# A fused two-layer decoder trunk: most columns of the first feed-forward matrix by rows, transposed by a transfer instead of by TensorE

## The chip, the cores and the metric

The kernel runs on one core of one Trainium2 chip. The metric is device time in microseconds (us) for one execution of the whole program, weights read from HBM. TensorE is called PE in the profile, VectorE DVE, ScalarE ACT, GpSimd POOL and SyncE SP. L223 is line 223 of the kernel before; a name ending in q (ACTq) is an engine's instruction queue issuing a transfer.

## The reference

256 tokens of width 1024 go through two layers. Each layer is a feed-forward half-step, a mixer (spatial gating and differential attention) and a second feed-forward half-step, with a layer norm after each:

```python
def _swiglu(x, w1, w3, w2):
    return (jax.nn.silu(x @ w1) * (x @ w3)) @ w2
...
for l in range(DEPTH):                                   # DEPTH = 2
    h = _swiglu(x, ffn_w1[l, 0], ffn_w3[l, 0], ffn_w2[l, 0])
    x = _layernorm(ALPHA * x + 0.5 * h, ln_g[l, 0], ln_b[l, 0])
    h = _mixer(x, l, w_in[l], ...)
    x = _layernorm(ALPHA * x + h, ln_g[l, 1], ln_b[l, 1])
    h = _swiglu(x, ffn_w1[l, 1], ffn_w3[l, 1], ffn_w2[l, 1])
    x = _layernorm(ALPHA * x + 0.5 * h, ln_g[l, 2], ln_b[l, 2])
```

The inner width of the feed-forward networks (FFNs) is 2816, 22 tiles of 128 columns. There are four FFNs in all. Only their first product, `silu(x @ w1) * (x @ w3)`, and what depends on its layout is touched here.

## The kernel before

Every fp32 product is made of three products of reduced parts: an operand is split into a high part (`ACT` copies it into a rounded type, L169 for weights and L176 for activations) and a low part (`DVE` subtracts, L171 and L177), and PE computes hi x hi, hi x lo and lo x hi into one PSUM bank. Weights come from HBM in 1 MB tiles `raw` (4 slots, transfers issued by SP) and are split in pieces of 128x1024 into `hi` and `lo` slots (8 of each), so that PE has up to eight pieces waiting for it. PSUM has four main banks (`bank`) and four side banks (`side_bank`, `sbank` in the profile), each set taken in turn.

A first product is computed in one of two ways.

- By columns (`gemm_a2`, L223 and L230): the weight tile is the stationary operand, the moving one is `x_cat`, all 256 tokens with high and low parts side by side, 512 wide; then the low weights against the high half, 256 wide. The result stands with the inner columns on partitions, which is what the product with `w2` needs. For each of the four banks of a pair of column tiles ACT copies the second half of the bank out (`r`, L231), and DVE adds the first half to it (L233); then follow silu (L599), the product (L603 or L607) and the split.
- By rows (`gemm_first` or `gemm_b2`, with `rows_b` and `three`, L211): 128 tokens of x are stationary, 512 columns of weights move, three products each. One block of four column tiles is 96 such matmuls. The result stands with tokens on partitions and has to be transposed: `front` computes silu and product for one half `t` of the tokens, and `turned` transposes it on PE, four matmuls against the identity (L585), into a side bank, from which it is split.

Before the change, column tiles 0 to 3 come by rows and tiles 4 to 21 by columns, in nine pairs.

The product with `w2` follows (the w2 stage). Four of the pairs of tiles, `SQ` = (4,5), (6,7), (8,9), (10,11), go through a Strassen-like scheme: `mixed` makes sums of the activations, `stream_s` sums of the weights (`shi`, `slo`; L293, L295, L306 to L309), and seven products `S[1]` to `S[7]` are accumulated, three matmuls each, S[3], S[7] and S[4] in side banks and the others in main banks. The rest, `PQ`, is multiplied plainly and accumulated into the same banks and one more side bank. After the first pair's seven products a plain pair follows, and so on.

Order: PE's instructions are issued as the program writes them. On ACT, DVE, POOL and SP a scheduler sorts the work by due times that it derives from PE's program (`step`, `beat` advance that clock; `beside(g, n)` puts a generator's work n units later in it), and the result is a fixed order: an engine that waits for one instruction does not run the next one. Transfers that an engine issues stand in the same order.

Of the kernel before, what the change touches and what calls it, by code (L numbers as in the profile page):

```python
# [12 lines left out]
F32R = mybir.dt.float32r  # L13
BF16 = mybir.dt.bfloat16
I32 = mybir.dt.int32
AF = mybir.ActivationFunctionType
ALU = mybir.AluOpType
AX = mybir.AxisListType

P = 128  # L20
D = 1024
T = 256
# [31 lines left out]
def trunk(ctx, tc, x, xT, w13a, w13b, w2s, w2p, wb, wqk, wa, wbr, wo, gateb, sgug, sgub, sguwT, sgubias, lam, diffg,  # L54
# [81 lines left out]
    def beside(task, delay):  # L136
        tasks.append([clock[0] + delay, task])
# [72 lines left out]
        for n, (w, xx) in enumerate([(w_hi, xh), (w_lo, xh), (w_hi, xl)]):  # L210
            PE.matmul(ps, xx, w, start=start and n == 0, stop=stop and n == 2)  # L211

    def gemm_a2(srcs, xc, zs, rs=lambda: s512("r"), scale=1.0):

        b, got = [], []
        for src in srcs:
            got += stream(src)
            for hi, _ in got[-2:]:  # L220
                b.append(bank())
                for k in range(KT):
                    PE.matmul(b[-1], hi[:, k * P : (k + 1) * P], xc(k), start=k == 0, stop=False)  # L223
                beat(0.65)
        for n, (_, lo) in enumerate(got):
            s = slice(n % 2 * T, (n % 2 + 1) * T)
            if n % 2 == 0:
                r, z = rs(), zs(n // 2)
            for k in range(KT):
                PE.matmul(b[n][:, :T], lo[:, k * P : (k + 1) * P], xc(k)[:, :T], start=False, stop=k == KT - 1)  # L230
            emptied[0] = A.activation(r[:, s], b[n][:, T:], AF.Copy, scale=scale).ins  # L231
# [85 lines left out]
    def gemm_b2(srcs, xh, xl, done, norm=None):  # L317
# [233 lines left out]
    def ffn(l, f, i, norm, last=False):  # L551
        xh, xl = parts(both)
        h_hi, h_lo = ({q: act.tile([P, 512], F32R, tag="slot", name=name(n)) for q in PQ} for n in ("hhi", "hlo"))
        f_hi, f_lo = ([d[k, k + 1] for k in range(0, FB, 2)] for d in (h_hi, h_lo))
# [21 lines left out]
        def front(t, ps):  # L576
            s = t512("silu")
            A.activation(s, ps[0], AF.Silu)
            V.tensor_tensor(out=s, in0=s, in1=ps[1], op=ALU.mult)
            beside(turned(t, s), 2)  # L580

        def turned(t, s):
            b = side_bank()
            for k in range(FB):
                PE.transpose(b[:, k * P : (k + 1) * P], s[:, k * P : (k + 1) * P], ident)  # L585
            b4 = b.rearrange("p (k t) -> p k t", k=4)
            for j in range(2):
                hi, lo = (v.rearrange("p (k t) -> p k t", k=2)[:, :, t * P : (t + 1) * P] for v in (f_hi[j], f_lo[j]))
                split(hi, lo, b4[:, 2 * j : 2 * j + 2])
            yield 0  # L590

        if norm is None:
            gemm_first([w13b[l, f, 0], w13b[l, f, 1]], front)
        else:
            gemm_b2([w13b[l, f, 0], w13b[l, f, 1]], xh, xl, front, norm=norm)
        for j in range(FB, FT, 2):
            for m, z in gemm_a2([w13a[l, f, j - FB + m] for m in range(2)], both, lambda m: t512("silu")):
                s = z[:, :T]
                silu[0] = A.activation(s, s, AF.Silu).ins  # L599
                if (j, j + 1) in SQ:  # L600
                    if m == 0:
                        qa = s512("qa")
                    V.tensor_tensor(out=qa[:, m * T : (m + 1) * T], in0=s, in1=z[:, T:], op=ALU.mult)  # L603
                    if m:
                        mixed((j, j + 1), qa)
                else:
                    V.tensor_tensor(out=s, in0=s, in1=z[:, T:], op=ALU.mult)  # L607
                    split(hh(j + m), hl(j + m), s)
                if norm is None and j + m == FB:
                    beside(setup(s[:, :1]), 0)  # L610
        ln = Norm(l, i, 2.0 * ALPHA, 4.0 * EPS, s[:, :1], last)
# [46 lines left out]
    def mixer(l, i, norm):  # L658
# [34 lines left out]
        def attend(hp, qT, kT):  # L693
# [7 lines left out]
            def exps(t):  # L701
# [7 lines left out]
                pp = []  # L709
                for m in range(2):  # L710
                    o = m * 4 + t * 2
                    p = s512("pp", 4)[:, : 2 * nk]
# [118 lines left out]
        def spatial(gp, uu):  # L831
            b = side_bank()
            for j in range(2):
                g = gp * 2 + j
                s = slice((g % 4) * P, (g % 4 + 1) * P)
                for t in range(NT):
                    PE.matmul(b[:, j * T + t * P : j * T + (t + 1) * P], vg[t][:, g // 4, s], wsT[g // 4][:, s],  # L837
                               start=True, stop=True)
            s1 = s512("sgu", 4)
# [51 lines left out]
def _layout(i):  # L891
# [30 lines left out]
    nb = FB * P  # L922
    w1, w3 = f["ffn_w1"], f["ffn_w3"]
    o["w13a"] = c(np.stack([cols(w1[..., nb:]), cols(w3[..., nb:])], axis=4)).reshape(L, 2, FT - FB, P, CH)
    o["w13b"] = c(np.concatenate([halves(w1[..., :nb]), halves(w3[..., :nb])], axis=2))
    w2 = f["ffn_w2"].reshape(L, 2, FT, P, 2, 512)

    def blocks(at):
# [45 lines left out]
```

## Time and profile before

| | |
|---|---|
| time, median of three runs | 1230.99 us (1230.78 to 1231.02) |
| the profiled execution's own time | 1231.23 us |
| its span in the profile | 1229.5 us |
| PE busy | 1223.3 us, 99%, 6589 matmuls |
| DVE busy | 980.3 us, 80% |
| ACT busy | 781.1 us, 64% |
| POOL busy | 87.0 us, 7% |
| moved by transfers | 241.87 MB, mean 197 GB/s |
| granted PE clock | full in all 40 slices |

The profile is one execution. Busy times are shares of the span; the chain of waits names the work that ended last at each moment; a windows view cuts the span into stretches. In the FFNs' rows a pair of column tiles appears as 32 matmuls of L223 and 32 of L230, a block by rows as 96 of L211.

### The profile page before, as it was taken

Reading aid. Unit: us, or ns where it says so; the run is one execution under the profiler, and the core shown is the slowest. Engines: PE = TensorE matmul, PEld = TensorE weight load, DVE = VectorE, ACT = ScalarE, POOL = GpSimd, SP = SyncE. Lnnn points to the kernel's source line nnn. Section 1 sums busy time; section 2 is a strip of 40 time slices with the busy share of each in tenths; the row PEclk is TensorE's granted clock in tenths of the full one; section 3 lists DMA queues with packets and bytes.
Section 4 is the critical chain, followed back from the end, with each engine's and each line's share of the span. In section 5 each row is a group of like instructions: output and inputs, shape, how many; then the busy total and the mean of one; then the engine's idle time right before and its main releaser. Section 6 shows DMA issues by size and latency. Waiting matters only on the chain.

```text
span 1229.5 us, 17890 instructions
## 1 busy us (share of the span) xinstructions
PE 1223.3 (99%) x6589; PEld 1050.6 (85%) x6589; DVE 980.3 (80%) x1692; ACT 781.1 (64%) x1424; POOL 87.0 (7%) x184
## 2 busy tenths in 40 slices
PE   9999999999999999999999999999999999999998
PEld 8888888888888888888888888888888888888886
DVE  6877998886587987779978779978866879787886
ACT  6775666679665666656566665566886555766651
POOL 0100000244100000000000000002430000000000
PEclk9999999999999999999999999999999999999999
DMA  9864665654754745546645546656556446455450
GB/s 344 291 205 138 231 217 194 224 167 166 251 178 154 231 159 207 191 138 241 247 178 196 180 142 247 246 188 206 168 174 229 168 171 240 171 206 178 160 211 34
DMA packets 40104, 241.87 MB, mean 197 GB/s; under 512 B 5281, under 2 KB 6353, under 8 KB 13393
## 3 DMA queue, kind: packets, MB, share of 16 engines
q1 hardware_dynamic: 36048, 227.82, 53.2%
q0 software_dynamic: 3536, 12.13, 3.1%
q8 instruction: 51, 0.84, 0.3%
q10 hardware_dynamic: 432, 0.79, 0.2%
q14 instruction: 37, 0.30, 0.1%
HBM read 235.47 MB, written 1.05 MB: 192 GB/s over the span
## 4 chain that ended last, share of the span: by engine, by line
PE 99%; DMA 0%; DVE 0%; ACT 0%; DVEq 0%; issue 0%; ACTq 0%
PE bank L223 38%; PE bank L211 23%; PE bank L230 20%; PE sbank L211 12%; PE bank L371 2%; PE sbank L707 1%; PE sbank L532 1%; PE sbank L756 1%; PE sbank L837 1%; DMA xraw<-in_xT 0%; PE sbank L754 0%; PE sbank L778 0%; PE sbank L585 0%; PE sbank L741 0%; PE sbank L746 0%; PE sbank L504 0%
## 5 line engine op out<-in xcount | busy, mean ns | idle before, releaser
L171 DVE TENSOR_TENSOR wlo<-raw,whi 128x1024 fp32r<-128x1024 f32 (+1 forms) x410 | 450.0, 1116 | 109.1 <-PE bank L230 62.9
L169 ACT ACTIVATE whi<-raw 128x1024 fp32r<-128x1024 f32 (+1 forms) x410 | 388.8, 970 | 186.9 <-PE bank L223 114.8
L223 PE MATMUL bank<-x,whi 128*128 128x512 f32 x1792 | 426.5, 392 | 0.0
L223 PEld LDWEIGHTS bank<-x,whi 128*128 128x128 f32 x1792 | 330.7, 188 | 69.1 <-issue 2.7
L230 PE MATMUL bank<-x,wlo 128*128 128x256 f32 x1792 | 230.0, 284 | 0.0
L230 PEld LDWEIGHTS bank<-x,wlo 128*128 128x128 f32 x1792 | 224.2, 191 | 4.8
L231 ACT ACTIVATE r<-bank 128x256 f32<-128x256 f32 x256 | 96.0, 381 | 67.8 <-PE bank L230 67.4
L211 PE MATMUL bank<-whi,x 128*128 128x512 f32 x328 | 106.6, 394 | 0.0
L293 ACT ACTIVATE shi<-raw 128x1024 fp32r<-128x1024 f32 (+1 forms) x64 | 60.4, 950 | 61.0 <-DVE raw L309 39.1
L295 DVE TENSOR_TENSOR slo<-raw,shi 128x1024 fp32r<-128x1024 f32 (+1 forms) x64 | 69.3, 1088 | 24.8 <-PE bank L230 15.3
L211 PEld LDWEIGHTS bank<-whi,x 128*128 128x128 f32 x328 | 61.6, 188 | 12.7
L211 PE MATMUL sbank<-whi,hhi 128*128 128x512 f32 x168 | 65.7, 391 | 0.0
L211 PE MATMUL sbank<-whi,hlo 128*128 128x512 f32 x168 | 65.4, 389 | 0.0
L211 PE MATMUL sbank<-wlo,hhi 128*128 128x512 f32 x168 | 65.4, 389 | 0.0
L211 PE MATMUL bank<-wlo,x 128*128 128x512 f32 x164 | 64.0, 390 | 0.0
L538 ACT ACTIVATE xf<-sbank,ln_b,ln_g 128x128 f32<-128x128 f32 x80 | 30.1, 456 | 40.8 <-PE sbank L532 40.8
L233 DVE TENSOR_TENSOR silu<-bank,r 128x256 f32<-128x256 f32 x144 | 54.5, 418 | 0.4
L431 POOL DMA_DIRECT2D bc<-in_lng x6 | 3.2, 530 | 728.4 <-DVE bc L430 728.4
L683 POOL TENSOR_TENSOR swap<-swap,sin_t 128x512 f32<-128x512 f32 x16 | 25.0, 1563 | 233.4 <-DMA swap<-z 225.2
L211 PE MATMUL bank<-lhi,x 128*128 128x512 f32 x120 | 39.2, 395 | 0.0
L211 PEld LDWEIGHTS sbank<-whi,hlo 128*128 128x128 f32 x168 | 31.5, 188 | 6.7
L211 PEld LDWEIGHTS sbank<-wlo,hhi 128*128 128x128 f32 x168 | 31.6, 188 | 6.5
(236 smaller groups left out, 1682.3 us busy)
## 6 DMA issues: line engine op xcount, KB each, us to landing
raw<-in_w13a SPq DMA_DIRECT2D x72, 1024.0 KB, 4.9
raw<-in_w2p SPq DMA_DIRECT2D x28, 1024.0 KB, 5.1
raw<-in_wa SPq DMA_DIRECT2D x24, 1024.0 KB, 5.2
raw<-in_w2s SPq DMA_DIRECT2D x16, 1024.0 KB, 4.9
raw<-in_wb SPq DMA_DIRECT2D x16, 1024.0 KB, 5.0
raw<-in_wqk SPq DMA_DIRECT2D x16, 1024.0 KB, 5.2
raw<-in_wbr SPq DMA_DIRECT2D x16, 1024.0 KB, 4.9
raw<-in_w13b SPq DMA_DIRECT2D x12, 1024.0 KB, 5.1
```

Of the source, the lines that this page charges most:

```text
L169: A.activation(h, r, AF.Copy)
L171: V.tensor_tensor(out=w, in0=r, in1=h.bitcast(F32), op=ALU.subtract)
L211: PE.matmul(ps, xx, w, start=start and n == 0, stop=stop and n == 2)
L223: PE.matmul(b[-1], hi[:, k * P : (k + 1) * P], xc(k), start=k == 0, stop=False)
L230: PE.matmul(b[n][:, :T], lo[:, k * P : (k + 1) * P], xc(k)[:, :T], start=False, stop=k == KT - 1)
L231: emptied[0] = A.activation(r[:, s], b[n][:, T:], AF.Copy, scale=scale).ins
L233: a = V.tensor_tensor(out=z[:, s], in0=b[n][:, :T], in1=r[:, s], op=ALU.add)
L293: A.activation(h, r, AF.Copy)
L295: V.tensor_tensor(out=w, in0=r, in1=h.bitcast(F32), op=ALU.subtract)
L371: PE.matmul(ps[t][m], x[:, j, o + t * P : o + (t + 1) * P], y, start=k0 + j == 0 and o == 0 and y is hi, stop=k0 + j == KT - 1 and y is lo)
L538: A.activation(xf[:, s], b[:, s], AF.Identity, scale=self.gT[:, f], bias=self.bT[:, f])
L683: turned_by[0] = G.tensor_tensor(out=s3, in0=s3, in1=s, op=ALU.mult).ins
```

## The change

Now 20 of the 22 column tiles come by rows: five blocks of 512 columns, `gemm_first` or `gemm_b2` for block 0 and the new `gemm_rows` for blocks 1 to 4, whose four banks alternate between the side banks (blocks 1 and 3) and the main banks (blocks 2 and 4). Only the pair (20, 21) still comes by columns, in side banks.

The result of a half block is no longer transposed on PE. A transposing transfer handles 16-bit elements, so ACT copies the fp32 result into two planes of 512 16-bit halves (`planes`, L603 of the changed kernel), ACT's queue issues a transposing transfer of 128x1024 16-bit elements, 256 KB, from SBUF to SBUF (`turned`, L606), and ACT's second copy joins the planes again (`columns`, L614), with `beside(..., 4)`. Behind the second half's join the block's two pairs of tiles go to `mixed` or to a split. There are ten such transfers in each FFN, 40 in all.

Besides, the seven products come in the order 1, 2, 5, 6, 3, 7, 4 instead of 3, 7, 4, 1, 2, 5, 6; the pool of activation slots has 28 instead of 31; the tag `side` of the 512-wide temporaries has 5 buffers instead of 4; one buffer `columns` is added; the scratch of dynamic transfers is 4096 instead of 8192; and the host's layout of `w1` and `w3` follows the blocks.

```diff
+NB = 5
+FR = NB * FB
...
-    act = ctx.enter_context(tc.tile_pool(name="act", bufs=31))
+    act = ctx.enter_context(tc.tile_pool(name="act", bufs=28))
...
-    def s512(s, n=4):
+    def s512(s, n=5):
...
-    def gemm_a2(srcs, xc, zs, rs=lambda: s512("r"), scale=1.0):
+    def gemm_a2(srcs, xc, zs, rs=lambda: s512("r"), scale=1.0, bank=bank):
...
+    def gemm_rows(srcs, xh, xl, done, bank):
+        ps = [[bank() for _ in range(2)] for _ in range(NT)]
+        for c in range(2):
+            for m in range(2):
+                for i, piece in enumerate(stream(srcs[m][:, c * CH : (c + 1) * CH])):
+                    for t in range(NT):
+                        rows_b(ps[t][m], t, 4 * c + 2 * i, piece, xh, xl, KT)
+        for t in range(NT):
+            done(t, ps[t])
...
-        def turned(t, s):
-            b = side_bank()
-            for k in range(FB):
-                PE.transpose(b[:, k * P : (k + 1) * P], s[:, k * P : (k + 1) * P], ident)
...
+        def keep(q, qa):
+            if q in SQ:
+                mixed(q, qa)
+            else:
+                split(p_hi[q], p_lo[q], qa)
+
+        def front(k0, first=False):
+            got = []
+            def rows(t, ps):
+                s, pk = t512("silu"), s512("planes").bitcast(U16)
+                A.activation(s, ps[0], AF.Silu)
+                V.tensor_tensor(out=s, in0=s, in1=ps[1], op=ALU.mult)
+                A.activation(pk.rearrange("p (w k) -> p w k", w=2), s.bitcast(U16).rearrange("p (k w) -> p w k", w=2),
+                             AF.Copy)
+                tt = s512("turned").bitcast(U16)
+                A.dma_start_transpose(out=tt.rearrange("p (c t) -> p c t", c=2 * FB), in_=pk)
+                beside(columns(t, tt), 4)
+
+            def columns(t, tt):
+                if not got:
+                    got.append(tmp.tile([P, 2, 512], F32, tag="columns", name=name("columns"), bufs=1))
+                h = got[0]
+                to = h.bitcast(U16).rearrange("p q (k u t w) -> p (q k) u t w", k=2, u=2, w=2)[:, :, t]
+                A.activation(to, tt.rearrange("p (w c t) -> p c t w", w=2, c=FB), AF.Copy)
+                if t == NT - 1:
+                    for j in range(2):
+                        keep((k0 + 2 * j, k0 + 2 * j + 1), h[:, j])
...
-        for j in range(FB, FT, 2):
+        for n in range(1, NB):
+            gemm_rows([w13b[l, f, m, n] for m in range(2)], xh, xl, front(n * FB), (bank, side_bank)[n % 2])
+        for j in range(FR, FT, 2):
...
-            for b in (3, 7, 4, 1, 2, 5, 6):
+            for b in (1, 2, 5, 6, 3, 7, 4):
...
-    nc = bacc.Bacc("TRN2", target_bir_lowering=False, num_devices=1, dynamic_dma_scratch_size=8192)
+    nc = bacc.Bacc("TRN2", target_bir_lowering=False, num_devices=1, dynamic_dma_scratch_size=4096)
```

How the work stands in order at the end of the column stage of the first FFN, on ACT. Before, these are ACT's instructions from the last S weight pieces made ahead (`shi`) through the last pair's four `r` copies, in the main banks 1316, 1325, 1344 and 1353:

```order
L293 ACTIVATE shi_1440<-raw_1432 128x1024
L169 ACTIVATE whi_1476<-raw_1474 128x1024
L169 ACTIVATE whi_1480<-raw_1474 128x1024
L293 ACTIVATE shi_1510<-raw_1508 128x1024
L231 ACTIVATE r_1362<-bank_1316 128x256
L231 ACTIVATE r_1362<-bank_1325 128x256
L293 ACTIVATE shi_1512<-raw_1508 128x1024
L231 ACTIVATE r_1388<-bank_1344 128x256
L599 ACTIVATE silu_1363<-silu_1363 128x256
L231 ACTIVATE r_1388<-bank_1353 128x256
```

After the change (line numbers are the changed kernel's; `r` is L234), from block 4's planes on, with the last pair in side banks 1091, 1100, 1119 and 1128:

```order
L603 ACTIVATE planes_1067<-silu_1066 128x1024
L172 ACTIVATE whi_1256<-raw_1254 128x1024
L606 DMA_TRANSPOSE turned_1071<-planes_1067 128x8x128
L603 ACTIVATE planes_1074<-silu_1073 128x1024
L172 ACTIVATE whi_1260<-raw_1254 128x1024
L606 DMA_TRANSPOSE turned_1078<-planes_1074 128x8x128
L614 ACTIVATE columns_1183<-turned_1071 128x4x256
L296 ACTIVATE shi_1290<-raw_1288 128x1024
L234 ACTIVATE r_1137<-sbank_1091 128x256
L614 ACTIVATE columns_1183<-turned_1078 128x4x256
L234 ACTIVATE r_1137<-sbank_1100 128x256
L634 ACTIVATE silu_1138<-silu_1138 128x256
```

The two transposing transfers and the two joins that wait for them now stand ahead of the `r` copies of the last pair; behind these rows follow a split, a weight piece, a split and the third `r` (from side bank 1119).

On PE, at the start of the w2 stage, before (the first matmul of each S product and the last of the pair ahead):

```order
L230 MATMUL bank_1353<-x_130,wlo_1341 128x256 x4
L211 MATMUL sbank_1424<-shi_1436,shh_505 128x512
L211 MATMUL sbank_1425<-shi_1438,shh_505 128x512
L211 MATMUL sbank_1426<-shi_1440,shh_504 128x512
L211 MATMUL bank_1427<-shi_1434,shh_504 128x512
```

and after, where 1204, 1205 and 1206 are the side banks that held 1091, 1100 and 1119:

```order
L233 MATMUL sbank_1128<-x_130,wlo_1116 128x256 x4
L214 MATMUL bank_1207<-shi_1214,shh_625 128x512
L214 MATMUL bank_1208<-shi_1216,shh_625 128x512
L214 MATMUL bank_1209<-shi_1218,shh_626 128x512
L214 MATMUL bank_1210<-shi_1220,shh_626 128x512
L214 MATMUL sbank_1204<-shi_1216,shh_626 128x512
L214 MATMUL sbank_1205<-shi_1218,shh_626 128x512
L214 MATMUL sbank_1206<-shi_1220,shh_625 128x512
```

Before, the pair's main banks were taken over by the fourth to seventh product; now its side banks are taken over by the fifth to seventh, and the main banks that block 4 used by the first four.

More of the change, by code (lines that the diff above doesn't have):

```diff
@@ L15 @@
 I32 = mybir.dt.int32
+U16 = mybir.dt.uint16
 AF = mybir.ActivationFunctionType
@@ L553, in ffn @@
         h_hi, h_lo = ({q: act.tile([P, 512], F32R, tag="slot", name=name(n)) for q in PQ} for n in ("hhi", "hlo"))
-        f_hi, f_lo = ([d[k, k + 1] for k in range(0, FB, 2)] for d in (h_hi, h_lo))
+        p_hi, p_lo = h_hi, h_lo
         h_hi, h_lo = ({k: d[q][:, j * T : (j + 1) * T] for q in PQ for j, k in enumerate(q)} for d in (h_hi, h_lo))
@@ L574, in mixed @@
                        for n, j, c in ((1, 0, 0), (2, 0, 2), (4, 0, 3), (7, 1, 0), (5, 1, 1), (6, 1, 2), (3, 1, 3))}
[L576 to L580, printed above, removed]
-        def turned(t, s):
-            b = side_bank()
-            for k in range(FB):
[L585 to L590, printed above, removed]
+        def keep(q, qa):
[3 more added lines that the diff above has]
+                split(p_hi[q], p_lo[q], qa)
@@ new lines, in front @@
+        def front(k0, first=False):
[18 more added lines that the diff above has]
+                        keep((k0 + 2 * j, k0 + 2 * j + 1), h[:, j])
+                    if first:
+                        beside(setup(h[:, 0, :1]), 0)
+                yield 0
+            return rows
@@ L592, in ffn @@
         if norm is None:
-            gemm_first([w13b[l, f, 0], w13b[l, f, 1]], front)
+            gemm_first([w13b[l, f, 0, 0], w13b[l, f, 1, 0]], front(0, True))
         else:
-            gemm_b2([w13b[l, f, 0], w13b[l, f, 1]], xh, xl, front, norm=norm)
-        for j in range(FB, FT, 2):
-            for m, z in gemm_a2([w13a[l, f, j - FB + m] for m in range(2)], both, lambda m: t512("silu")):
+            gemm_b2([w13b[l, f, 0, 0], w13b[l, f, 1, 0]], xh, xl, front(0), norm=norm)
+        for n in range(1, NB):
+            gemm_rows([w13b[l, f, m, n] for m in range(2)], xh, xl, front(n * FB), (bank, side_bank)[n % 2])
@@ L598, in ffn @@
+        for j in range(FR, FT, 2):
+            qa = s512("qa")
+            for m, z in gemm_a2([w13a[l, f, j - FR + m] for m in range(2)], both, lambda m: t512("silu"), bank=side_bank):
                 s = z[:, :T]
                 silu[0] = A.activation(s, s, AF.Silu).ins
[L600 to L608, printed above, removed]
@@ L609, in ffn @@
-                if norm is None and j + m == FB:
-                    beside(setup(s[:, :1]), 0)
-        ln = Norm(l, i, 2.0 * ALPHA, 4.0 * EPS, s[:, :1], last)
+                V.tensor_tensor(out=qa[:, m * T : (m + 1) * T], in0=s, in1=z[:, T:], op=ALU.mult)
+            keep((j, j + 1), qa)
+        ln = Norm(l, i, 2.0 * ALPHA, 4.0 * EPS, qa[:, :1], last)
         S = {n: side_bank() for n in (3, 7, 4)}
@@ L711, in exps @@
                     o = m * 4 + t * 2
-                    p = s512("pp", 4)[:, : 2 * nk]
+                    p = s512("pp")[:, : 2 * nk]
                     for j in range(2):
@@ L838, in spatial @@
                                start=True, stop=True)
-            s1 = s512("sgu", 4)
+            s1 = s512("sgu")
             bias = bsb[gp // 2][:, (gp % 2) * T : (gp % 2 + 1) * T].rearrange("p (j t) -> p j t", j=2)
@@ L920, in halves @@
         return w.reshape(*w.shape[:-2], (k // P) * 512)
-    nb = FB * P
+    nb = FR * P
     w1, w3 = f["ffn_w1"], f["ffn_w3"]
-    o["w13a"] = c(np.stack([cols(w1[..., nb:]), cols(w3[..., nb:])], axis=4)).reshape(L, 2, FT - FB, P, CH)
-    o["w13b"] = c(np.concatenate([halves(w1[..., :nb]), halves(w3[..., :nb])], axis=2))
+    o["w13a"] = c(np.stack([cols(w1[..., nb:]), cols(w3[..., nb:])], axis=4)).reshape(L, 2, FT - FR, P, CH)
+    o["w13b"] = c(np.stack([halves(w1[..., :nb]), halves(w3[..., :nb])], axis=2))
     w2 = f["ffn_w2"].reshape(L, 2, FT, P, 2, 512)
```

## The prediction

> **What bounds the kernel now.** I read the page first: busy time, the clock row and the chain of waits. Then I read the chain's rows inside one feed-forward network (FFN), and last what the other engines and the transfers do there.
>
> ```profile
> span 1229.5 us, 17890 instructions
> PE 1223.3 (99%) x6589; PEld 1050.6 (85%) x6589; DVE 980.3 (80%) x1692; ACT 781.1 (64%) x1424; POOL 87.0 (7%) x184
> PEclk9999999999999999999999999999999999999999
> PE 99%; DMA 0%; DVE 0%; ACT 0%; DVEq 0%; issue 0%; ACTq 0%
> ```
>
> TensorE is busy for 1223.3 of 1229.5 us at a clock that is never throttled, and the chain that ends last is TensorE from end to end. So a microsecond of matmul that is removed is a microsecond gained, as long as the other engines keep feeding TensorE; and a microsecond that TensorE waits for them is lost in full. VectorE's 80% and ScalarE's 64% cost nothing as they stand. These rows of the chain price the matmuls (start, length, line, count):
>
> ```profile
> 316.98 21.79 PE bank L211 x96
> ...
> 449.19 0.44 PE sbank L585 x4
> ...
> 544.45 7.28 PE bank L223 x32
> 551.73 3.83 PE bank L230 x32
> 555.56 2.07 PE sbank L211 x9
> ...
> 588.23 8.16 PE bank L211 x36
> ```
>
> The first row is a whole block of 96 matmuls by rows (226.98 ns each; the last row, 8.16/36, gives 226.7). The L585 row is the four transposes of one half of such a block's result. The L223 and L230 rows are one pair of column tiles by columns: 7.28 + 3.83 = 11.11 us.
>
> **What the change takes from TensorE.** A block by rows covers four column tiles, as two pairs do. In each FFN eight pairs (8 x 11.11 = 88.88 us) become four blocks (4 x 21.79 = 87.16 us): 1.72 us less, 6.9 us over four FFNs. The transposes of L585 go: two groups of four for each FFN, 8 x 0.44 = 3.5 us. Together 10.4 us of TensorE time. The row price could only be off by the 0.3 ns between the two rows above, times 4 x 384 matmuls: 0.4 us.
>
> **What it adds elsewhere.** For each block and each half of 128 tokens: on ScalarE a 1024-element copy (the planes), a transposing transfer of 256 KB from SBUF to SBUF issued from ScalarE's queue, and a second 1024-element copy (the join). For each two pairs it takes away eight `r` copies, eight VectorE additions and halves the number of silu and product steps, which become twice as long. How full the two engines are, by the windows view over all column pairs, over two of them (22.2 us), and over the stage behind them:
>
> ```profile
> core 0: us, PE busy (x) PEld busy (x) DVE busy (x) ACT busy (x) POOL busy (x), PEclk, DMA share, GB/s
> 455.10:555.60 100.50, 100.50 (x582) 89.04 (x581) 77.83 (x125) 64.34 (x108) 0.00 (x0) 1.00 0.55 186
> 488.60:510.80 22.20, 22.20 (x130) 19.66 (x129) 17.83 (x31) 14.71 (x24) 0.00 (x0) 1.00 0.56 190
> 555.60:588.00 32.40, 32.40 (x144) 26.81 (x143) 28.84 (x36) 17.84 (x22) 1.05 (x2) 1.00 0.70 256
> ```
>
> Durations of the operations, from ScalarE's timeline and then VectorE's (start, length, operation; the distance from one start to the next is what an engine pays):
>
> ```profile
> 24.51 0.58 ACT L578 ACTIVATE silu<-bank 128x512 f32<-128x512 f32 x1
> 25.01 2.01 ACT L169 ACTIVATE whi<-raw 128x1024 fp32r<-128x1024 f32 x2
> 550.80 1.99 ACT L169 ACTIVATE whi<-raw 128x1024 fp32r<-128x1024 f32 x2
> 552.70 1.04 ACT L293 ACTIVATE shi<-raw 128x1024 fp32r<-128x1024 f32 x1
> 553.64 0.64 ACT L231 ACTIVATE r<-bank 128x256 f32<-128x256 f32 x2
> 25.97 0.68 DVE L579 TENSOR_TENSOR silu<-silu,bank 128x512 f32<-128x512 f32 x1
> 26.57 2.35 DVE L171 TENSOR_TENSOR wlo<-raw,whi 128x1024 fp32r<-128x1024 f32 x2
> ```
>
> ScalarE: 0.95 us for 1024 elements, 0.50 for 512, 0.3 for 256; VectorE: 0.60 for 512, 1.14 for 1024 (2.28 for two in the row that follows in the same view). The 16-bit copies have no row; 512 elements bound one from below (0.50), two passes of 1024 from above (1.9); I take 0.95, the row of the same element count. A block in the middle then holds on ScalarE 8 weight copies (7.6), 2 activations (1.0), 2 planes and 2 joins (3.8), 4 splits (2.0), so 14.4 us plus two issues in 21.79. That is where it was before (14.71 of 22.20). VectorE loses some 3.5 us in each block. Eight weight pieces are buffered ahead of TensorE, a block's worth of 21.79 us, and cost ScalarE 7.6 us to refill; so inside a block it may wait some 13 us for one transfer before TensorE notices. All of this is costed at nothing, hidden under 21.79 us of matmuls; without that cover it would be the wait itself, once for each block.
>
> **The one place without that cover** is the end of block 4. Call its last matmul time 0. TensorE then does the last column pair (hi part to 7.28, its four banks finished at 8.24, 9.2, 10.15 and 11.11), then twelve matmuls in the new order S[1], S[2], S[5], S[6] (12 x 0.2267 = 2.72, to 13.83), then S[3] at 13.83, S[7] at 14.5, S[4] at 15.2. These three write into the very side banks that the last pair has just filled, so they need ScalarE's `r` copies and VectorE's additions out of them; and ScalarE, which works in a fixed order, has both halves' planes, transfers and joins ahead of those copies. With c for the time in which ScalarE is held by an issue and L from issue to landing:
>
> - weight piece to 1.2; planes 1 to 2.2; weight piece to 3.14; transfer 1 issued; planes 2 to 4.1 + c; weight piece to 5.07 + c; transfer 2 issued;
> - join 1 at the later of 5.07 + 2c and 3.14 + L, 0.95 long; a piece of S weights, 0.95; the first `r` copy, not before 8.24, so done at about 8.74;
> - join 2 at the later of 8.74 and 5.07 + c + L; then the second `r`, silu, two splits, a weight piece and the third `r` (0.3 + 0.3 + 1.0 + 0.95 + 0.3, and two hand-overs from VectorE of some 0.5), to about 13.6; VectorE's split, product, split and addition put S[4]'s bank free at about 14.4.
>
> S[4] wants it at 15.2: 0.8 us to spare. The stall is what c + L has above 4.5 us (3.67 to reach 8.74, and the 0.8), or, for a long issue, 2(c - 0.72) - 0.8, whichever is more. It comes four times. The gain of 10.4 is eaten at 2.6 us for each FFN: c + L of 7.1, or c of 2.4.
>
> No transposing transfer is in this trace. The nearest rows are the transfers between two places in SBUF, the only ones from ScalarE's queue, and their issue times (min/median/max in ns):
>
> ```profile
> swap<-z SPq DMA_DIRECT2D x64, 64.0 KB, 2.5
> out_x<-xtok ACTq DMA_DIRECT2D x2, 256.0 KB, 2.1
> raw<-in_w13b ACTq DMA_DIRECT2D x1, 256.0 KB, 4.0
> raw<-in_w13a SPq DMA_DIRECT2D x72, 1024.0 KB, 4.9
> L679 SPq DMA_DIRECT2D swap<-z x64: 507/588/1457, 216.0 to 872.6; - x64
> DMA to landing us min/median/max: 1.9/2.5/6.5
> L513 ACTq DMA_DIRECT2D out_x<-xtok x2: 338/343/348, 1216.0 to 1226.2; - x2
> ```
>
> From below: c 0.34 and L 2.1. From above: c 1.46 and L 6.5. I take the swap's median, a transfer of the same kind: c 0.59, and 2.5 us plus what 192 KB more take by the difference of the 1 MB and 64 KB rows (192/960 x 2.4 = 0.5), so L 3.0. c + L is 3.6: no stall. The sum is 1231.23 - 10.4 = 1220.8 us, against the profiled execution (1229.5 span and 1.73 around it), which lies 0.24 above the median of the runs, 1230.99, less than I can resolve.
>
> The rest is neutral. The 28 slots of the activation pool and the smaller scratch of dynamic transfers touch loads that POOL issues some 40 us ahead of use, with POOL busy 7%. The transposes add 2.6 MB for each FFN, some 24 GB/s over a stage that moves 186 at a DMA share of 0.55.
>
> [...] The swap rows say 2.5 us for a whole 64 KB. [...]
>
> **The rivals.**
> 1. *The transfer lands later, but not by much.* c + L between 4.8 and 6.5 (the loads' 4.9 us at 0.6 of issue is 5.5): 0.3 to 2.0 us of stall in each FFN, 1222 to 1229; at 5.5, 1224.8. For it: a DMA share of 0.55 to 0.70 there. Against: the swaps' median. Below that lies the break-even case, 1228.5 to 1233.5.
> 2. *Slower: the transposes go one after another, and ScalarE, held by its join, copies the last pair's banks too late.* Place: the start of the w2 stage, S[3], S[7] and S[4] in a reused side bank. With the slowest swap (1.46 and 6.5 side by side) c + L is 8.0, 3.5 us in each FFN: 1234.8. With the second transfer behind the first, it lands at 3.14 + 13.0 = 16.1, 7.4 after 8.74, less 0.8: 6.6 us each, 1247. It decides from c + L = 7.1. [...] Against: the ordinary SBUF transfers' medians.
> 3. *The change doesn't do what it says on TensorE*: rows no faster than columns, because a block's banks are refilled sooner than its activations read them, and only the transposes are saved: 1231.23 - 3.5 = 1227.7. Against: the 21.79 row is a block with just such a hand-over, and two sets of banks now alternate.
>
> **How the numbers follow.** The forecast (no stall, 1219.5 to 1222.5) has 0.52; rival 1 has 0.12 below the break-even; rival 3 has 0.03; the break-even zone 0.08; rival 2 has 0.25, since nothing of this trace shows the new transfer and only 3.5 us of c + L separate forecast and loss. A measurement of this kernel tells 0.2%, 2.5 us, from no change. Faster is 0.52 + 0.12 + 0.03 = 0.67, the same 0.08, slower 0.25. The likeliest one's own range is 1219 to 1223; the range over all cases is 1218.5 to 1243, which leaves out a little of the good side and the worst of rival 2.
>
> **What would show it.** L211 blocks of 21.8 us in place of eight L223/L230 pairs in the chain, and no L585 rows; the transposing transfer's own issue time and landing (right below 4.5 us in sum); between the last pair and S[4] no idle TensorE. Wrong would be: TensorE idle ahead of S[3] to S[4] with ScalarE's join or `r` copy as releaser, an issue above 2.4 us, or a TensorE clock or weight load that suffers from the transposes' traffic.

## The result and the profile after

The changed kernel takes 1270.14 us (median of four runs, 1268.19 to 1271.74) against 1231.01 before: ratio 1.0318, 95% interval 1.0300 to 1.0335. It is slower by 39 us, where 1220.8 was forecast, and lies above the range. Its profiled execution has a span of 1268.9 us.

From the page of the changed kernel: span, busy times, granted clock, queues (packets, MB, share) and the chain of waits by engine.

```profile
span 1268.9 us, 16510 instructions
PE 1230.1 (97%) x6045; PEld 1026.3 (81%) x6045; DVE 933.2 (74%) x1504; ACT 801.3 (63%) x1316; POOL 87.4 (7%) x184
PEclk9999799999999999998999998999999999999999
q1 hardware_dynamic: 36048, 227.82, 51.2%
q10 hardware_dynamic: 42672, 11.28, 6.6%
PE 54%; issue 22%; DVE 9%; DMA 9%; ACT 5%; POOL 1%; DVEq 0%; ACTq 0%; POOLq 0%
```

TensorE runs 544 instructions fewer and is nevertheless busy for 6.8 us longer; it is idle for 38.8 us instead of 6.2; and its clock, full before, dips (in three slices of the row; four stretches of half clock are read below). These three make a ledger. The instructions that went are worth 10.4 us, as forecast (below), so TensorE should have been busy for 1212.9 us; it was busy for 17.2 us more, most of it at a lower clock, and idle for 32.6 us more: 17.2 + 32.6 - 10.4 = 39.4 us, the difference of the spans.

The new transfer, by the view of the tile it writes (duration of the issue in ns, then of the landing in us, min/median/max), and who waited for it longest (total us, times, longest):

```profile
L606 ACTq DMA_TRANSPOSE turned<-planes x40: 1247/1250/1891, 27.2 to 1190.7; - x40
DMA to landing us min/median/max: 2.7/6.4/13.9
ACT columns L614 <- DMA turned<-planes: 89.5, 20, 10.4
```

So c was 1.25 us, not 0.59, and L 6.4, not 3.0. ScalarE stood 89.5 us in front of its joins.

TensorE's idle times in the first FFN, by its timeline (start, length, operation; in brackets the idle time before it and who ended it), at the end of the column stage, the start of the w2 stage and its end:

```profile
117.67 6.12 PE L226 MATMUL sbank<-x,whi 128*128 128x512 f32 x24 [0.80 <-ACT whi L172]
...
131.82 0.48 PE L214 MATMUL bank<-shi,shh 128*128 128x512 f32 x1 [2.54 <-DVE silu L602]
...
142.03 0.79 PE L214 MATMUL sbank<-shi,shh 128*128 128x512 f32 x1 [7.35 <-DVE silu L236]
...
146.27 0.80 PE L214 MATMUL sbank<-shi,shh 128*128 128x512 f32 x1 [1.12 <-DVE silu L236]
...
184.80 0.50 PE L214 MATMUL bank<-wlo,hhi 128*128 128x512 f32 x1 [1.13 <-DVE wlo L174]
```

The long waits end with VectorE's addition out of a side bank (L236), the place that the prediction named. But there are others that it did not name: a product of block 4 (L602) that TensorE waits for in the first FFN, and a late weight piece at the end of the w2 stage. All four FFNs have a gap of the L236 kind: 7.35 and 1.12, 3.24 and 1.12, 4.06 and 1.11, 1.55 to 1.81 us. The w2 stage's end has 1.13, 1.39, 1.14 and 3.69 us.

Why that addition was late, by ScalarE's timeline from block 3's second half on (block 4 ends at 114.89):

```profile
107.42 1.62 ACTq L606 DMA_TRANSPOSE turned<-planes  x1
109.09 1.06 ACT L603 ACTIVATE planes<-silu 128x1024 uint16<-128x1024 uint16 x1 [1.70 <-issue]
...
115.49 1.18 ACT L614 ACTIVATE columns<-turned 128x1024 uint16<-128x1024 uint16 x1 [4.38 <-DMA turned<-planes]
...
123.73 0.63 ACT L296 ACTIVATE shi<-raw 128x512 fp32r<-128x512 f32 x1 [1.58 <-DMA raw<-in_w2s]
124.27 1.07 ACT L601 ACTIVATE silu<-bank 128x512 f32<-128x512 f32 x2
...
130.04 1.06 ACT L296 ACTIVATE shi<-raw 128x1024 fp32r<-128x1024 f32 x1 [2.66 <-DVE raw L312]
131.71 1.06 ACT L603 ACTIVATE planes<-silu 128x1024 uint16<-128x1024 uint16 x1 [0.62 <-DVE silu L602]
...
139.14 1.17 ACT L614 ACTIVATE columns<-turned 128x1024 uint16<-128x1024 uint16 x1 [3.04 <-DMA turned<-planes]
...
142.48 0.37 ACT L234 ACTIVATE r<-sbank 128x256 f32<-128x256 f32 x1
```

Read it downward. Block 3's join waits for its transfer until 115.49. The weight piece behind it (116.57), and VectorE's half of it (117.65), come late; only then is a `raw` slot free, and the S weights are requested at 118.90 and land 4.8 us later. The silu of block 4 stands in ScalarE's order behind a piece of these S weights, and block 4's product in VectorE's order behind more of them. So block 4's planes start at 131.71, 16.8 us after the block's end; the prediction had 1.2. In the second FFN it is 5.7 us (564.13 after 558.48). Where no transfer is waited for (experiment 1), they start 1.2 us after the block (115.81 after 114.64), as the prediction has it.

### The profile page after: what moved, and what is told of

Read it like the earlier page. It is cut to its first block, busy times and chain, and to the rows that moved or that the text cites. A ratio compares the mean times of both kernels' runs of the same rounds, so it can differ in the third digit from the quotient of the medians.

```text
span 1268.9 us, 16510 instructions
## 1 busy us (share of the span) xinstructions
PE 1230.1 (97%) x6045; PEld 1026.3 (81%) x6045; DVE 933.2 (74%) x1504; ACT 801.3 (63%) x1316; POOL 87.4 (7%) x184
## 3 DMA queue, kind: packets, MB, share of 16 engines
q10 hardware_dynamic: 42672, 11.28, 6.6%
## 4 chain that ended last, share of the span: by engine, by line
PE 54%; issue 22%; DVE 9%; DMA 9%; ACT 5%; POOL 1%; DVEq 0%; ACTq 0%; POOLq 0%
PE bank L214 16%; PE sbank L214 15%; PE bank L226 12%; PE bank L233 6%; DMA turned<-planes 6%; DVE wlo L174 3%; DVE slo L298 2%; PE bank L385 2%; ACT whi L172 1%; DMA raw<-in_w2s 1%; ACT columns L614 1%; PE sbank L733 1%; ACT shi L296 1%; DVE xtok L479 1%; DMA bc<-in_lng 1%
## 5 line engine op out<-in xcount | busy, mean ns | idle before, releaser
L174 DVE TENSOR_TENSOR wlo<-raw,whi 128x1024 fp32r<-128x1024 f32 (+1 forms) x410 | 449.3, 1119 | 170.5 <-ACT whi L172 131.8
L214 PE MATMUL bank<-whi,x 128*128 128x512 f32 x840 | 264.7, 390 | 0.0
L214 PEld LDWEIGHTS bank<-whi,x 128*128 128x128 f32 x840 | 157.7, 188 | 32.6
L214 PE MATMUL bank<-wlo,x 128*128 128x512 f32 x420 | 163.6, 390 | 0.0
L214 PE MATMUL sbank<-whi,x 128*128 128x512 f32 x512 | 158.9, 389 | 0.0
L226 PE MATMUL bank<-x,whi 128*128 128x512 f32 x640 | 158.3, 395 | 0.0
L226 PEld LDWEIGHTS bank<-x,whi 128*128 128x128 f32 x640 | 116.5, 188 | 25.9 <-issue 2.7
L214 PEld LDWEIGHTS sbank<-whi,x 128*128 128x128 f32 x512 | 96.1, 188 | 20.0
L614 ACT ACTIVATE columns<-turned 128x1024 uint16<-128x1024 uint16 x40 | 47.0, 1175 | 89.5 <-DMA turned<-planes 89.5
L214 PE MATMUL sbank<-wlo,x 128*128 128x512 f32 x256 | 99.6, 389 | 0.0
L233 PE MATMUL bank<-x,wlo 128*128 128x256 f32 x640 | 85.8, 285 | 0.0
L233 PEld LDWEIGHTS bank<-x,wlo 128*128 128x128 f32 x640 | 81.6, 191 | 2.3
L603 ACT ACTIVATE planes<-silu 128x1024 uint16<-128x1024 uint16 x40 | 42.2, 1054 | 30.7 <-DVE silu L602 11.6
L234 ACT ACTIVATE r<-bank 128x256 f32<-128x256 f32 x112 | 41.9, 380 | 27.5 <-PE bank L233 27.5
```

The source lines that it names most:

```text
L174: V.tensor_tensor(out=w, in0=r, in1=h.bitcast(F32), op=ALU.subtract)
L603: A.activation(pk.rearrange("p (w k) -> p w k", w=2), s.bitcast(U16).rearrange("p (k w) -> p w k", w=2), AF.Copy)
L614: A.activation(to, tt.rearrange("p (w c t) -> p c t w", w=2, c=FB), AF.Copy)
```

## The experiments

Experiments 1 to 6, 9 and 10 are single executions. The four of the changed kernel lie within 3.6 us and the ten of experiment 7 within 6.9, so a difference of a few us between two of them counts only where the traces show the gaps that make it.

**1. No transfer.** The join reads the planes.

```diff
-                tt = s512("turned").bitcast(U16)
-                A.dma_start_transpose(out=tt.rearrange("p (c t) -> p c t", c=2 * FB), in_=pk)
-                beside(columns(t, tt), 4)
+                beside(columns(t, pk), 4)
```

> The transposing transfer is left out: the join reads the planes directly, so each FFN's rows come out untransposed; every other step of the change stays. Theory A (the transfer: its landing, 6.4 us median and up to 13.9, holds ScalarE at the join, and weight pieces, S weights and the last pair's r copies queue behind it; then TensorE's clock is halved after the gap): no transfer, no gap, so the forecast of 1219 to 1223 us, or up to 1226 if the gap at the end of the w2 stage stays. Theory B (the issue, 1.25 us of ScalarE's queue each): the same here. Theory C (not the transfer: the two 1.05 and 1.17 us copies, the new order of S, fewer activation slots): 1255 to 1270.

Measured: 1226.78 us, beside 1231.38 for the kernel before. No gap at the start of the w2 stage, and no dip of the clock:

```profile
span 1224.7 us, 16457 instructions
PE 1213.8 (99%) x6045; PEld 1020.8 (83%) x6045; DVE 936.1 (76%) x1504; ACT 804.1 (66%) x1316; POOL 86.7 (7%) x184
166.72 0.50 PE L214 MATMUL bank<-wlo,hhi 128*128 128x512 f32 x1 [1.14 <-DVE wlo L174]
```

The transfer costs 43 of the change's microseconds. TensorE is busy for 1213.8 us with the same 6045 matmuls as the changed kernel, against 1212.9 worked out: the forecast of what leaves TensorE holds, and what the changed kernel has above it is mostly clock. The two copies fit beside the weight pieces; theory C falls as the cause of the 39 us. What is left above 1221 stands mostly at the end of the w2 stage, in all four FFNs (1.14 us three times and 1.50).

**2. An ordinary transfer of the same size.**

```diff
-                A.dma_start_transpose(out=tt.rearrange("p (c t) -> p c t", c=2 * FB), in_=pk)
+                A.dma_start(tt, pk)
```

> An ordinary transfer of the same 256 KB, SBUF to SBUF, from ScalarE's queue in the transposing one's place, so the rows are moved but not transposed. Theory A in the form that transposing is what is slow: issue about 0.34 us and landing about 2.5 to 3 us, time 1219 to 1226. Rival (any transfer of that size lands late beside the weight loads): landing 5 us and more, time 1245 to 1270. Theory C: 1255 to 1270.

Measured: 1241.78 us, between the two expectations.

```profile
L606 ACTq DMA_DIRECT2D turned<-planes x40: 472/472/528, 26.9 to 1164.4; - x40
DMA to landing us min/median/max: 2.2/3.9/8.2
q10 hardware_dynamic: 6192, 11.27, 2.6%
```

The shortest landing is 2.2 us, but the median is 3.9 and the longest 8.2. So it isn't transposing alone: an ordinary transfer on this queue is late at times too. The queue's count is 6192 packets here and 42672 with the transposes (432 of them without either transfer, in experiment 1): some 144 packets for a transfer against 1056, and with the sevenfold count the median grew from 3.9 to 6.4.

**3. The transposes on SyncE's queue.**

```diff
-                A.dma_start_transpose(out=tt.rearrange("p (c t) -> p c t", c=2 * FB), in_=pk)
+                nc.sync.dma_start_transpose(out=tt.rearrange("p (c t) -> p c t", c=2 * FB), in_=pk)
```

> The transposing transfer is issued from SyncE's queue instead of ScalarE's; nothing else. Theory A (landing): ScalarE still waits at the join, 1260 to 1275. Theory B (ScalarE held by issues): 1222 to 1240.

Measured: 1247.20 us, between the expectations, and for a reason that neither had: the landing itself changed.

```profile
L606 SPq DMA_TRANSPOSE turned<-planes x40: 1237/1238/2258, 27.0 to 1167.7; - x40
DMA to landing us min/median/max: 2.7/3.4/8.3
ACT columns L614 <- DMA turned<-planes: 41.7, 30, 3.0
```

The same transfer with the same issue time lands in 3.4 us (median) where the weight loads stand in the same queue, and in 6.4 beside them in another. That made a new form of theory A: a transfer on ScalarE's queue lands late because it shares the transfer engines with the loads of SyncE's queue. In the changed kernel's own trace the landing does go with the loads. In the second FFN the first transpose has the engines to itself (issued at 466.32; the next load is issued at 468.57) and lands in 2.7 us; the 96 GB/s over that stretch are its own 256 KB. In the first FFN one is issued at 54.17, behind loads that SyncE issued at 44.70, 46.97 and 49.24 and beside one of 54.80, and lands in 13.9. The third row is the time ahead of it, the fourth a part of it, and the last is from experiment 2, with two ordinary copies beside a load:

```profile
466.32:469.05 2.73, 2.73 (x14) 2.26 (x13) 2.73 (x3) 2.12 (x3) 0.00 (x0) 1.00 0.43 96
54.17:68.06 13.89, 13.89 (x63) 11.51 (x62) 1.83 (x2) 2.01 (x2) 0.00 (x0) 1.00 1.17 159
50.00:55.00 5.00, 5.00 (x24) 4.14 (x23) 3.56 (x4) 3.07 (x3) 0.00 (x0) 1.00 1.02 428
56.00:65.00 9.00, 9.00 (x41) 7.48 (x40) 1.23 (x1) 1.63 (x2) 0.00 (x0) 1.00 1.17 57
...
53.00:60.00 7.00, 7.00 (x33) 5.79 (x32) 2.90 (x3) 3.05 (x3) 0.00 (x0) 1.00 0.98 373
```

(Stretch and its length, then the engines' busy times; the last three numbers are the clock, the DMA share and GB/s.) The landings agree with the new form: 2.7 us for 1056 packets with no other on the engines, 13.9 beside loads. In that stretch packets of both queues run together: from 55 to 58 us 795 of ScalarE's queue (0.20 MB) and 55 of SyncE's (0.32 MB). In what order an engine takes them is not shown; that they take turns, as the expectation of experiment 7 has it, is a supposition that no run tested by itself.

Sharing is not all, though. The ordinary copies land late (7.5 us, median of the two, and the load in 8.0) while the engines go on moving 373 GB/s. Beside the two transposes the engines move 57 GB/s for nine us, after 428, with a DMA share of 1.17, and the load of 54.80 itself takes 13.0 us to land, where the median is 5.1. In this stretch the transposes and the load are slow together. Why stays open, and so does how much of the median of 6.4 is due to it.

**4. Block 4's joins behind the last pair's `r` copies.**

```diff
-                beside(columns(t, tt), 4)
+                beside(columns(t, tt), 4 if k0 < FR - FB else 5)
...
-                A.activation(to, tt.rearrange("p (w c t) -> p c t w", w=2, c=FB), AF.Copy)
+                with behind(emptied[0] if k0 == FR - FB else None):
+                    A.activation(to, tt.rearrange("p (w c t) -> p c t w", w=2, c=FB), AF.Copy)
```

> Block 4's two joins and their splits stand behind the last pair's r copies on ScalarE; blocks 0 to 3 unchanged. Theory A: the gaps before S[3], S[7] and S[4] (1.1 to 7.4 us) and most of the half clock behind them go; what block 3's join delays (weight pieces, S weights, block 4's product in the first FFN) stays: 1233 to 1246. Rival (the r copies are late for another reason, the S weights ahead of them): 1262 to 1270.

Measured: 1258.16 us, between the two: 12 us better than the change, half of the least that theory A expected. The gap ahead of S[3] in the first FFN is still 5.07 us, in the second 3.31: the late planes and the second of the two issues remain ahead of the `r` copies, and the planes are late for the reason read above.

**5. No transfer, and the old order for the last seven products.**

```diff
-            for b in (1, 2, 5, 6, 3, 7, 4):
+            for b in (3, 7, 4, 1, 2, 5, 6) if n == NS - 1 else (1, 2, 5, 6, 3, 7, 4):
```

> As the first experiment (the transfer left out, rows untransposed), and the last of the four pairs takes its seven products in the old order 3, 7, 4, 1, 2, 5, 6. Theory D: the first experiment ended at 1226.8 instead of 1221 because in the new order S[1] and S[7] are read at other moments, so VectorE's last weight pieces come 1.1 to 1.5 us late at the end of the w2 stage, and ScalarE and TensorE with them; then these gaps are gone here: 1220.5 to 1223.5. Rival (those late pieces come from the smaller activation pool or from the denser loads, not from the order): 1225.5 to 1227.5.

Measured: 1220.04 us, beside 1230.92. The gaps at the end of the w2 stage are gone, and the chain is TensorE alone again:

```profile
span 1218.1 us, 16458 instructions
PE 1211.6 (99%) x6045; PEld 1020.4 (84%) x6045; DVE 935.1 (77%) x1504; ACT 803.7 (66%) x1316; POOL 86.7 (7%) x184
PE 99%; DMA 0%; DVE 0%; ACT 0%; DVEq 0%; issue 0%; ACTq 0%
```

Theory D holds here: the new order of S, which the prediction put down to nothing at the stage's end, cost 6.7 us (1226.78 to 1220.04), 4.9 of it in the four gaps. With that order S[1] and S[7] are finished at other times, and VectorE's additions from them stand ahead of its last weight pieces (in the first FFN six of them from 160.12 to 163.80 in experiment 1, ahead of the piece of 165.45; in experiment 5 they start at 163.31). And this run, without the transfer but with the smaller pool and scratch that the prediction called neutral, comes to the forecast's 1220.8.

**6. Experiment 4 with the old order for the last seven products** (the edits of 4 and 5 together).

> Block 4's joins behind the r copies as in the fourth experiment, and the old order for the last seven products; the transposes still from ScalarE's queue. Theory D with theory A: some 3 to 8 us under the fourth experiment's 1258: 1250 to 1256. If the order does nothing: 1256 to 1260.

Measured: 1250.04 us, 8 us less than experiment 4, at the edge of what theory D with theory A expected. No gap is left at the end of a w2 stage.

**7. SyncE's queue, block 4's joins last, the old order for the last products** (the edits of 3, 4 and 5).

> The transposes issued from SyncE's queue, where they stand in line with the weight loads instead of sharing the engines with them, block 4's joins behind the r copies, the old order for the last seven products. Theory A in its new form (the landing is long because the loads of the other queue take turns with it): the third experiment's gaps in the first FFN (3.7, 2.6 and 0.7 us) and the half clock behind them go, and the w2 stage's end too: 1221 to 1228. Rival (SyncE's wait for the planes makes loads late): 1235 or more.

Measured: 1226.22 us (1224.53 to 1231.44) against 1230.92; ratio 0.9965 (0.9954 to 0.9976). Two gaps at a w2 stage's start are left, 2.40 us in the first FFN and 0.57 in the last. The rival, loads starved by SyncE's waits, would have been 1235 or more.

**8. The same, with a block's two transposes next to each other.** Loads of later blocks are issued behind both.

```diff
+        with behind(hold[0]):
-        nc.sync.dma_start(raw[:, :width], src)
+            nc.sync.dma_start(raw[:, :width], src)
...
+            hold[0] = sent.get(n - 2)
```

(`sent[n]` is the last transpose of block n; the last pair of columns uses block 2's, the plain pairs of the w2 stage block 3's.)

> As the seventh, and both transposes of a block stand next to each other on SyncE's queue, ahead of the load that stood between them. Theory A in its new form: the second one's landing falls from about 6.3 to about 3 us; TensorE hardly waited there any more, so the time is that of the seventh or up to 3 us less: 1220 to 1226. Rival (loads that start 2 to 3 us later starve a block's first weight pieces): 1228 or more.

Measured: 1222.96 us (1222.51 to 1224.90) against 1230.92; ratio 0.9937 (0.9922 to 0.9952). This version is 0.6% below the kernel before.

```profile
span 1221.1 us, 16552 instructions
PE 1213.1 (99%) x6045; PEld 1020.3 (84%) x6045; DVE 936.3 (77%) x1504; ACT 806.5 (66%) x1316; POOL 87.0 (7%) x184
L610 SPq DMA_TRANSPOSE turned<-planes x40: 1231/1239/2181, 26.5 to 1146.7; - x40
DMA to landing us min/median/max: 2.7/2.8/7.9
131.45 0.50 PE L216 MATMUL sbank<-shi,shh 128*128 128x512 f32 x1 [1.61 <-DVE silu L238]
```

With no load between them, the transposes land in 2.8 us (median), close to the 2.7 of one alone. The 1.61 us are the only gap left at the start of a w2 stage.

**9. Issued as in the change, but nobody computes with what lands.**

```diff
-                beside(columns(t, tt), 4)
+                beside(columns(t, pk), 4)
```

> The transposing transfers are issued from ScalarE's queue as in the change, with the same issue time and traffic, but the join reads the planes, so nothing computes with what lands and the rows come out untransposed. Theory A (what costs is ScalarE's wait for the landing): the first experiment's 1226.8, up to 1230. Theory B (what costs is the issue, 40 times 1.25 us on ScalarE, or the traffic beside the loads): 1240 to 1265.

Measured: 1236.09 us, between the two. Of the 43 us by which the change stands above experiment 1, 34 go with the joins' wait for the landing. The other 9.3 are an upper bound for issue and traffic, because the experiment did not take all waiting away: a buffer that the transfer writes is reused, and VectorE waited for that. Whether TensorE lost by this wait is not shown.

```profile
DVE qb L576 <- DMA turned<-planes: 17.3, 7, 9.2
```

**10. The change with only the old order for the last products.**

> The change with nothing but the old order for the last pair's seven products. Theory D: the gaps at the end of the w2 stage go (1.1 to 3.7 us in each FFN, 7.4 in all), the gaps at its start stay: 1261 to 1265. Rival (in the change these gaps come from late loads): 1268 to 1272.

Measured: 1270.31 us: nothing gained, against the expectation; the rival's range has the number, but not by its reason. The four gaps at the w2 stage's end are gone, as theory D says, but those at its start summed to 28 us instead of 24 (7.10 us in the second FFN, where it was 3.24), and ahead of it the first FFN has 3.5 us of gaps, where the change has 0.8, with landings up to 15.8 us. Late transposes make the gaps depend on which loads they meet; whether this shift has a cause in the order or is such a meeting stays open.

**11. Experiment 8 with block 4's joins back ahead of the `r` copies.**

> The eighth experiment with block 4's joins back ahead of the last pair's r copies. With a landing of about 3 us the prediction's own sum for the w2 stage's start says no stall, so if landing alone decides: 1222 to 1226, as the eighth. If the place of the joins decides even with a short landing (the planes are late, since VectorE's products of block 4 stand behind S weights): gaps ahead of S[3] and S[7], 1228 to 1240.

Measured: 1225.88 us (1225.44 to 1227.89) against 1231.25; ratio 0.9956 (0.9939 to 0.9973). The time is the one expected if landing alone decides; but only three of the four FFNs have no gap, and the first has one of 4.94 us, as the other expectation says: there a transpose of block 3 held ScalarE for 5.59 us, and block 4's planes started 3.92 us later than ScalarE was ready for them, behind VectorE. With a short landing the prediction's chain at the end of block 4 does hold in three FFNs with the joins where the change has them.

## Why the prediction was wrong

**What leaves TensorE** was right: 10.4 us by the rows of the matmuls. Experiments 1, 5 and 8 have 1211.6 to 1213.8 us of TensorE for 1212.9 worked out; experiment 5's 1220.04 us is the sum as it was made, without a stall, though with the old order of the last products. Rival 3 falls with it: a block by rows took 21.76 to 21.79 us in the changed kernel too.

**c and L were mis-sized.** c was taken at 0.59 from the swaps' median and was 1.25, inside its bounds (0.34 to 1.46). L was taken at 3.0 and was 6.4, at the upper bound of 6.5, with single ones up to 13.9, far outside it. The first step that failed is L, by the choice of its row: the swap is a transfer of the same kind, but on SyncE's queue, where loads stand in line with it. In experiment 8, on that queue, L is 2.8. The only rows on ScalarE's queue were the last stores, when no load ran any more (2.1), and one load at the start (4.0). None had a second queue full of weight loads beside it, and the bound did not allow for that. Nor is the transfers' traffic neutral, as the prediction put it: in the stretch of experiment 3's rows a load took 13.0 us beside them. A transposing transfer with nothing beside it landed nearly as fast as the fastest ordinary one (2.7 against 2.2 us, experiment 2); its issue was longer (1.25 against 0.47).

**The sum for the w2 stage's start was incomplete.** With the measured c and L the prediction's own formula gives c + L - 4.5 = 3.2 us in each FFN, 1233.4 us: past rival 2's turning point (c + L is 7.65, beyond 7.1), at the top of the break-even zone, and still 37 us short. So the size of L alone does not explain the result. Three terms were missing.

- *The wait inside the blocks was costed at nothing, on a cover of 13 us.* That cover was counted in weight pieces of one block, and for these it held: TensorE's first gap in the changed kernel is at 117.67, behind block 4. But the wait was not only for weight pieces. ScalarE is busy for 14.6 of each 21.8 us (43.29 of 64.40 in the row below, nearly three blocks of the second FFN), and issues and waits for products come on top; by the end of block 4 it had not caught up. And what its wait holds back is not only the next piece but also the `raw` slot that the piece frees. The request for the S weights came late by that, and the silu and product of block 4 stand behind the S weights in ScalarE's and VectorE's fixed order. "Planes 1 to 2.2" was 16.8 + 1 us in the first FFN. Moving the joins alone (experiment 4) therefore gave only 12 us; the old order of the last products (6) gave 8 more, and shortening the landing on top of both (7, 8) the rest, 24 and 27 us.

```profile
471.60:536.00 64.40, 64.40 (x286) 53.33 (x285) 40.83 (x53) 43.29 (x52) 0.00 (x0) 1.00 0.76 224
```

- *The clock after a gap.* Nothing in the prediction has it, since the trace of before has no gap inside the FFNs. In the four stretches below, each behind a gap, most matmuls take 0.6 to 0.8 us instead of 0.39 and the granted clock is about half (start, end and length, TensorE's busy time with its matmuls, the clock, the DMA share and GB/s):

```profile
131.82:149.69 17.87, 9.32 (x21) 0.52 0.51 157
575.72:583.05 7.33, 6.07 (x14) 0.53 0.40 143
765.05:774.13 9.08, 7.97 (x17) 0.50 0.56 166
1241.61:1245.11 3.50, 3.50 (x9) 0.52 0.02 5
```

  These 61 matmuls were busy for 26.9 us; at the 0.227 us of the prediction's rows they would need 13.8. So some 13 of the 17.2 us are clock. The rest stays open. The gaps ahead are 2.54, 3.24, 4.06 and 3.69 us: in the first FFN the clock fell before the gap of 7.35 us, not after it. The length of a gap alone does not tell what follows. Behind one of 1.92 us in experiment 2 (566.59, with one of 0.36 us 3 us before it) five matmuls took 0.39 to 0.50 us, one 0.55 and then seven 0.63; behind one of 1.99 us in experiment 6 (571.81) all six before the next gap took 0.39 to 0.50; behind one of 2.22 us in experiment 9 (133.59) the first took 0.79 and the next five 0.63. So a gap of about 2 us may cost more than its length.
- *The new order of S.* It was looked at only where it helps, at the stage's start. At its end it cost 7.4 us of gaps in the change, and 6.7 us between experiments 1 and 5; undoing it in the change alone gained nothing (experiment 10).

Of the rivals, the second had mechanism and place (ScalarE held at its join, the last pair's banks copied late) and the right sign; its price, 3.5 to 6.6 us in each FFN, was a quarter to a half of the real one: 50 us over four FFNs, idle time and clock together, the end of the w2 stage included. Its "one after another" at 6.5 us each is not what happens where no load stands between the two: 2.8 us each in experiment 8 is against it.

## What to carry to other kernels

A transfer's landing depends on the traffic beside it and on its queue, not only on its size: here the same 256 KB landed in 2.7 us alone, in 6.4 beside the loads of another queue, and on the loads' own queue in 3.4, or in 2.8 with no load between a block's two (medians). Take the row from the same queue under the same load, and where many small packets meet large loads of another queue (here 1056 packets, all under 512 B, and loads of 1 MB), try the transfer in line with the loads. A wait on an engine with a fixed order is hidden only if everything behind it can be late, the buffers that it frees and what their next loads feed included; follow that loop once around (here block 4's planes started 16.8 us after the block instead of 1.2, experiment 1). And a gap on TensorE of about 2 us can cost its length and slow matmuls after it (behind 2.22 us in experiment 9 six of 0.63 to 0.79 us instead of 0.39).

## What the runs showed of the hardware

- A transposing transfer of 256 KB from SBUF to SBUF, of 16-bit elements (no other width was run), landed 2.7 us after its issue when nothing competed (the changed kernel at 466.32), and held the issuing queue for 1.25 us on ScalarE and 1.24 on SyncE (medians), against 0.47 us for an ordinary one of that size (experiment 2).
- On ScalarE such an issue ran beside an operation that had already started (issued at 110.18 for 1.25 us, beside the weight piece of 110.06 to 111.10), but the next one waited for it: 1.70 us of "issue" ahead of the second planes at 109.09.
- The same 40 transfers landed in 6.4 us (median) from ScalarE's queue beside the loads, 3.4 from SyncE's, and 2.8 there with no load between the two of a block.
- Two such transfers on ScalarE's queue and a load on SyncE's in flight together moved 57 GB/s for nine us (56 to 65 in the changed kernel), where two ordinary copies beside a load moved 373 (experiment 2, 53 to 60).
- TensorE's granted clock, 1.00 ahead of these gaps, was 0.50 to 0.53 in the stretches behind gaps of 2.54, 3.24, 4.06 and 3.69 us (the changed kernel), and 0.63 us matmuls followed gaps of 1.92 us (experiment 2) and 2.22 us (experiment 9), but not one of 1.99 us before the next gap (experiment 6).
